# A reordered hybrid encoder trunk: one token piece loaded by ScalarE, two diagonals made on ScalarE, the third input block in full width, and a new order table

## The chip, the cores and the metric

The kernel runs on one core of a Trainium2 chip. The metric is the device time of one execution in microseconds (us), lower is better. The times below are medians of several executions, and one execution was taken by the hardware profiler.

## What is computed

One layer of an encoder for 512 tokens of 1024 channels, in float32. In short, from the reference:

```python
h = rmsnorm(x, mix_norm)
p = h @ w_in                                  # 3072 + 3072 + 1024 + 32 + 2048 columns, cut in parts:
rx, ry, qkv, z, ba, gates = split(p)
y_rg = rglru_branch(rx, ry, ...)              # conv, gates r and i, a = exp(..r), scan both ways, * gelu(ry)
y_dn = deltanet_branch(qkv, z, ba, ...)       # conv, chunks of 64, triangular solve, state, gated norm, both ways
g = sigmoid(gates)
x = x + (g1 * (y_rg @ w_rnn_proj) + g2 * (y_dn @ w_dn_proj)) @ w_out
x = x + (silu(u) * v) @ w_down                # u, v = rmsnorm(x, ffn_norm) @ w_gate_up, D_FF = 2816
out = rmsnorm(x, final_norm)
```

Here rmsnorm multiplies every token by the reciprocal root of its mean square and every channel by a gain.

## The kernel before

**Layout and numbers.** Tokens are columns in most of the kernel: a matrix of channels by tokens. A float32 factor is split in a high part of fewer bits (type fp32r, made by a cast or a scaled copy) and the remainder, and a product is made of three products: high by high, high by low and low by high. For a block of 128 output channels of the input projection that makes 24 matrix products of 512 columns (`mm3`, 8 slices of 128 input channels by three), or, with `parts=2`, 48 products of 256 columns: first all 24 for one half of the tokens, then all for the other. Some large products (z, the gate and up projections, w_out) go by a scheme of seven products on sums of blocks in place of eight; the sums of weight blocks are made by a transfer that POOL (GpSimd) issues and that adds a block in memory to a tile (`t<-t` on POOL).

**Stages.** The tokens are loaded, squared, scaled by the gain and transposed on TensorE (PE). The first products, for z, use the tokens with the gain but without the reciprocal root, which is applied to the result. Meanwhile the roots are found: `rows_of` builds for each of the two token tiles of a pair a diagonal matrix of the reciprocal roots (ident times rin) and multiplies it by ones on PE, so that every partition holds the row of factors (tile r), which `scaled_parts` uses to make the normalised tokens hh (high) and hl (low). The first block that reads hh is the small block ba. Then follow the RG-LRU branch in four groups of three blocks of 128 channels (its last decay-gate ACTIVATE starts at 250 us), the DeltaNet branch in four groups of two heads, the output projections, the FFN and the final norm.

**What sets the order.** The kernel's functions don't emit instructions. V, A, G, T and Q are recorders (class `Rec`) of DVE (VectorE), ACT (ScalarE), POOL, PE and SP, and each call is noted with a number. `Plan.emit` then emits all recorded operations in the order of a long table of numbers, ORDER (lines 31 to 425); a second table, HOMES (lines 426 to 466), says which buffer each tile of the pools t2, t4 and ps gets, and a tile waits for the last use of what its buffer held. Every engine works through its own instructions in that order. Since all are emitted in one line, all rows of a profile of this kernel carry the line L517, and are told apart by the names and forms of their tiles.

**Names.** In the profile, t is any tile of the pools t2 and t4, ps a bank of the accumulators. With numbers, in the order: t211_88 and t212_89 are the first and the second half (512 channels each) of token tile 0, t213_90 and t214_91 those of token tile 1; t4522, t4525, t4530 and t4533 are weight pieces of z; t421 and t422 the first two high parts of the scaled tokens (without root), ps25 to ps28 the banks in which the tokens are transposed; t241 the diagonals; ps520 and ps521 the first results of z. Later t4582 is a weight block, t4583 and t4584 its cast and the cast's copy with the sign turned, which the in-memory sums use. Near the end ps1781 and ps1786 are 256-column quarters of the last result, ps1779 and ps1785 halves of 512 columns.

**Where the change sits.** The token loads go out on SP, the order of the loop is tile 0 first half, tile 1 first half, then the second halves, and the only transfer that ACT issues in the first microseconds is that of the gain. The squares of t211_88 and t213_90 are made by ACT, those of the second halves by DVE. `in_proj` is called for one block after another, counts them in `first_tiles`, and gives `mm3` two parts while fewer than three are done.

Of the kernel before, what the change touches and what calls it, by code (L numbers as in the profile page):

```python
# [9 lines left out]
AF = mybir.ActivationFunctionType  # L10
ALU = mybir.AluOpType
# [3 lines left out]
P = 128  # L15
# [507 lines left out]
def trunk(ctx: ExitStack, tc: tile.TileContext, x, mix_norm, w_in, rg_conv_w, rg_conv_b, rg_wa, rg_ba, rg_wx, rg_bx,  # L523
# [129 lines left out]
    def rows_of(rins):  # L653
        diag, pr, r = two(shape=(P, 2, P)), axb(), two(shape=(P, 256))
        for i, rin in enumerate(rins):
            V.tensor_scalar(diag[:, i, :], ident, rin, None, ALU.mult)
            T.matmul(pr[:, i * P:(i + 1) * P], ones, diag[:, i, :], start=True, stop=True)
# [1268 lines left out]
```

## Time and profile before

| what | value |
|---|---|
| median of 3 executions | 1045.61 us (1044.15 to 1045.66) |
| the profiled execution | 1045.31 us |
| its span in the trace | 1043.6 us |
| TensorE clock granted, mean | 0.999 |
| bytes read and written | 133.18 and 18.91 MB |
| instructions counted | 18109 |

Times in the profile are microseconds from the start of the span. A row of a timeline has the start, the duration, the engine, the line, the operation, the tiles (out<-in), the shapes and how many like it followed each other; in brackets stands how long the engine was idle before it and what it waited for. A row of the waits view gives the tile whose instruction waited, what was waited for, the total, the number and the longest. PEld is the weight load of TensorE, SPq, ACTq and POOLq are issues of transfers.

### The profile page before, as it was taken

The numbers are of one execution on the slowest core, as the hardware profiler recorded it, in microseconds if no ns is written. First come the engines' busy times: TensorE is split into PE (matmuls) and PEld (weight loads), VectorE is DVE, ScalarE is ACT, GpSimd is POOL, SyncE is SP. The second block draws the span as 40 slices with busy tenths as digits, with TensorE's granted clock in tenths as the row PEclk, the third lists the DMA queues.
The fourth block names the chain that finished last, engine by engine and source line by source line (L and its number), as shares of the span: only waits on it lengthen the run. The fifth ranks groups of instructions, "written<-read, shape, count | busy, mean of one in ns | idle before, by whom it ended". The sixth has DMA issues, their size and how long they took to land.

```text
span 1043.6 us, 18109 instructions
## 1 busy us (share of the span) xinstructions
PE 1031.2 (99%) x6699; PEld 902.5 (86%) x6699; DVE 909.2 (87%) x1701; ACT 726.7 (70%) x1325; POOL 97.5 (9%) x145
## 2 busy tenths in 40 slices
PE   8999999999999999999999999999999999999997
PEld 7988888888888898897788888889999999998886
DVE  6899999958986489768958969999999998999998
ACT  7789999898447567986987564678544454445674
POOL 6000000214000032241212000000000000000000
PEclk9999999999999999999999999999999999999999
DMA  9942523525515227898974645795473533265622
GB/s 288 310 158 87 165 76 84 132 70 150 128 51 158 57 70 208 203 206 202 274 182 106 173 138 188 249 302 180 144 240 122 152 87 87 80 202 161 221 102 81
DMA packets 185512, 163.75 MB, mean 157 GB/s; under 512 B 7728, under 2 KB 156352, under 8 KB 185424
## 3 DMA queue, kind: packets, MB, share of 16 engines
q1 hardware_dynamic: 178896, 144.63, 46.2%
q0 software_dynamic: 5344, 14.82, 7.8%
q10 hardware_dynamic: 1184, 3.15, 0.8%
q8 instruction: 52, 0.85, 0.3%
q14 instruction: 36, 0.29, 0.1%
HBM read 133.18 MB, written 18.91 MB: 146 GB/s over the span
## 4 chain that ended last, share of the span: by engine, by line
PE 87%; DMA 4%; ACT 4%; DVE 2%; issue 2%; SPq 0%; DVEq 0%; POOLq 0%; ACTq 0%
PE ps L517 87%; ACT t L517 3%; DMA t<-in_w_in_dram 2%; DVE t L517 2%; DMA t<-t 1%; ACT L517 1%; ACT ps L517 1%; DMA zs<-t 0%; SPq L517 0%; DVE na L517 0%; ACT drt L517 0%; ACT rst L517 0%; DVEq L1921 0%; DVE rin L517 0%; POOLq L517 0%
## 5 line engine op out<-in xcount | busy, mean ns | idle before, releaser
L517 PE MATMUL ps<-t,t 128*128 128x512 f32 (+3 forms) x3039 | 538.5, 321 | 2.2 <-DMA t<-t 1.4
L517 DVE TENSOR_TENSOR t<-t,t 128x512 fp32r<-128x512 f32 (+19 forms) x807 | 508.7, 662 | 35.2 <-PE ps L517 13.8
L517 PEld LDWEIGHTS ps<-t,t 128*128 128x128 f32 (+1 forms) x3039 | 432.4, 179 | 60.4 <-DMA t<-t 1.8
L517 PE MATMUL ps<-hh,t 128*128 128x512 f32 (+2 forms) x1696 | 459.0, 346 | 0.8 <-ACT t L517 0.6
L517 ACT CAST t<-t 128x512 fp32r<-128x512 f32 (+2 forms) x400 | 299.1, 781 | 169.2 <-DVE t L517 67.3
L517 PEld LDWEIGHTS ps<-hh,t 128*128 128x128 f32 (+1 forms) x1696 | 301.0, 189 | 40.7 <-ACT t L517 1.5
L517 PE MATMUL ps<-hl,t 128*128 128x512 f32 (+2 forms) x856 | 280.6, 346 | 0.0
L517 PEld LDWEIGHTS ps<-hl,t 128*128 128x128 f32 (+1 forms) x856 | 159.6, 188 | 18.6
L517 ACT ACT_TABLE_LOAD x69 | 88.5, 1283 | 5.9 <-DVE so L517 3.1
L517 DVE SCALAR_TENSOR_TENSOR t<-ps,par,t 128x511 f32<-128x511 f32 (+1 forms) x108 | 79.2, 744 | 11.2 <-ACT t L517 9.9
L517 ACT COPY t<-ps 128x512 f32<-128x512 f32 (+3 forms) x108 | 44.5, 429 | 56.3 <-PE ps L517 51.2
L517 ACT ACTIVATE t<-t 128x128 f32<-128x128 f32 (+5 forms) x114 | 72.6, 647 | 7.3 <-DVE t L517 6.2
L517 DVE TENSOR_TENSOR t<-ps,t 128x256 f32<-128x256 f32 (+1 forms) x106 | 50.7, 487 | 14.1 <-PE ps L517 12.3
L517 ACT ACTIVATE t<-ps,par 128x512 f32<-128x512 f32 x68 | 46.3, 705 | 10.0 <-PE ps L517 9.4
L517 DVE TENSOR_TENSOR t<-t 128x512 f32<-128x512 f32 (+1 forms) x81 | 51.4, 643 | 0.3
L517 ACT ACTIVATE t<-ps 128x512 f32<-128x512 f32 (+1 forms) x58 | 29.3, 509 | 23.4 <-PE ps L517 21.7
L517 PE MATMUL ps<-t,na 128*128 128x128 f32 (+2 forms) x640 | 44.2, 232 | 0.1
L517 PEld LDWEIGHTS ps<-t,na 128*128 128x128 f32 (+2 forms) x640 | 40.0, 145 | 3.8 <-issue 1.6
L517 POOL TENSOR_SCALAR_AFFINE_SELECT t<-t 128x512 f32<-128x512 f32 x32 | 24.7, 777 | 193.1 <-DMA t<-gcr 168.2
L517 PE MATMUL ps<-ident,t 128*128 128x128 f32 (+1 forms) x200 | 31.8, 275 | 1.3 <-DMA t<-in_x_dram 0.7
L517 POOL TENSOR_SCALAR t<-t,dnse 128x128 f32<-128x128 f32 x48 | 29.5, 768 | 38.9 <-ACT ps L517 23.9
L517 POOL DMA_DIRECT2D t<-t x20 | 17.4, 871 | 152.5 <-ACT t L517 129.0
(151 smaller groups left out, 598.3 us busy)
## 6 DMA issues: line engine op xcount, KB each, us to landing
t<-in_w_in_dram SPq DMA_DIRECT2D x70, 512.0 KB, 5.8
t<-in_w_gate_up_dram SPq DMA_DIRECT2D x44, 512.0 KB, 4.8
t<-in_w_down_dram SPq DMA_DIRECT2D x22, 512.0 KB, 5.1
t<-t POOLq DMA_DIRECT2D x20, 512.0 KB, 6.4
t<-in_w_down_dram SPq DMA_DIRECT2D x33, 256.0 KB, 3.9
t<-in_w_out_dram SPq DMA_DIRECT2D x12, 512.0 KB, 6.5
t<-in_w_rnn_proj_dram SPq DMA_DIRECT2D x16, 384.0 KB, 4.2
sums<-t SPq DMA_DIRECT2D x11, 512.0 KB, 5.6
```

The costliest lines, as they stand in the source:

```text
L517: self.plan.ops.append((self.eng, {x.tensor.name for x in aps}, outs, lambda: real(*a, **kw)))
```

## The change

Three functions are edited, and both tables are replaced.

```diff
@@ rows_of
         for i, rin in enumerate(rins):
-            V.tensor_scalar(diag[:, i, :], ident, rin, None, ALU.mult)
+            A.activation(diag[:, i, :], ident, AF.Copy, scale=rin)
             T.matmul(pr[:, i * P:(i + 1) * P], ones, diag[:, i, :], start=True, stop=True)
@@ trunk, the token loads
         for c in range(2):
-            Q.dma_start(xl_[c][h], x[0, c * P:(c + 1) * P, 512 * h:512 * h + 512])
+            (A if c and not h else Q).dma_start(xl_[c][h], x[0, c * P:(c + 1) * P, 512 * h:512 * h + 512])
@@ in_proj
-        mm3(po, hi, lo, lambda k: hh[:, k, :], lambda k: hl[:, k, :], KD, 2 if len(first_tiles) < 3 else 1)
+        mm3(po, hi, lo, lambda k: hh[:, k, :], lambda k: hl[:, k, :], KD, 2 if len(first_tiles) < 2 else 1)
@@ ORDER = """ (all numbers replaced; the first of each)
-2 17 18 19 20 21 22 23 24 25 26 27 28 29 0 3 5 2085 10 14 11 7 15 9 16 2086 1 12 13 66 67 6 2103 2104 2087 65 33 34 35
...
```

One of the four token loads, tile 1's first half, moves to ACT's queue. The two diagonals are made by ACT as a copy scaled by rin. The third block of the input projection is made with 24 products of 512 columns in place of 48 of 256. In number of instructions PE has 24 products fewer, DVE two operations fewer, ACT two ACTIVATEs, one transfer and four table loads more (73 for 69), SP one transfer fewer; the rest is the same work in another order and in other buffers. Lines of the changed kernel stand one lower, L516 for L517.

The head of SP's order, before and then now:

```order
L517 DMA t4522_599<-in_w_in_dram 128x512
L517 DMA t211_88<-in_x_dram 128x512
L517 DMA t213_90<-in_x_dram 128x512
L517 DMA t4522_599<-in_w_in_dram 128x512
L517 DMA t212_89<-in_x_dram 128x512
L517 DMA t214_91<-in_x_dram 128x512
```
```order
L516 DMA t4522_599<-in_w_in_dram 128x512 x2
L516 DMA t211_88<-in_x_dram 128x512
L516 DMA t4525_602<-in_w_in_dram 128x512
L516 DMA t212_89<-in_x_dram 128x512
L516 DMA t214_91<-in_x_dram 128x512
```

The second piece of the first weight moved ahead of the first token piece, a third weight piece ahead of the second halves, and t213_90 left this queue. The head of ACT's order, before and now:

```order
L517 DMA gain1r15_92<-in_mix_norm_dram 8x128
L517 ACT_TABLE_LOAD
L517 ACTIVATE warm10_87<-eps_t9_86 128x1
L517 CAST t4523_600<-t4522_599 128x512
L517 ACTIVATE t233_110,ssq29_106<-t211_88 128x512
L517 CAST t4523_600<-t4522_599 128x512
L517 ACTIVATE t421_98<-ps25_102,gain117_94 128x256
L517 ACTIVATE t239_116,ssq35_112<-t213_90 128x512
L517 ACTIVATE t421_98<-ps25_102,gain117_94 128x256
```
```order
L516 DMA t213_90<-in_x_dram 128x512
L516 DMA gain1r15_92<-in_mix_norm_dram 8x128
L516 ACT_TABLE_LOAD
L516 CAST t4523_600<-t4522_599 128x512
L516 ACT_TABLE_LOAD
L516 ACTIVATE warm10_87<-eps_t9_86 128x1
L516 CAST t4523_600<-t4522_599 128x512
L516 ACTIVATE t233_110,ssq29_106<-t211_88 128x512
L516 ACTIVATE t239_116,ssq35_112<-t213_90 128x512
L516 ACTIVATE t421_98<-ps25_102,gain117_94 128x256 x2
```

Both casts of the first weight and both squares now stand ahead of the first scaled half (t421). Further on in ACT's order the diagonals (t241) stand between scaled halves:

```order
L516 ACTIVATE rst37_114<-ssq35_112,ssh36_113 128x1
L516 ACTIVATE t241_118<-ident1_78,rin32_109 128x128
L516 ACTIVATE t422_99<-ps27_104,gain117_94 128x256
L516 ACTIVATE t241_118<-ident1_78,rin38_115 128x128
L516 CAST t4531_608<-t4530_607 128x512
```

On PE all sixteen transposes of the tokens stood ahead of the first product of z; now only the eight of t211_88 and t213_90 do, eight products follow, then the eight transposes of t212_89 and t214_91. In the middle (about 480 us), ACT's order around the cast and the copy of the weight block t4582, before and then now:

```order
L517 CAST t4583_660<-t4582_659 128x1024
L517 ACTIVATE t4584_661<-t4583_660 128x1024
L517 CAST t4593_670<-t4546_623 128x1024
L517 ACTIVATE t2770_847,so767_844<-t4736_813 128x128
L517 ACT_TABLE_LOAD
```
```order
L516 CAST t4583_660<-t4582_659 128x1024
L516 ACTIVATE t2770_847,so767_844<-t4736_813 128x128
L516 COPY t2850_927<-na841_918 32x256 x4
L516 COPY t4518_595<-ps551_628 128x512
L516 CAST t4591_668<-t4541_618 128x1024
L516 ACTIVATE t41056_1133<-t41055_1132 128x1024
L516 COPY t4518_595<-ps552_629 128x512
L516 ACTIVATE t2771_848,so767_844<-t4736_813 128x128
L516 ACTIVATE t2770_847,so767_844<-t4736_813 128x128
L516 ACTIVATE t4584_661<-t4583_660 128x1024
```

The copy t4584 stood right behind its cast; now eight rows stand between. The end of PE's order, before and now, the products of the down projection into the last banks:

```order
L517 MATMUL ps1786_1863<-t41971_2048,t41977_2054 128x256
L517 MATMUL ps1781_1858<-t41956_2033,t41960_2037 128x256
L517 MATMUL ps1781_1858<-t41955_2032,t41961_2038 128x256
L517 MATMUL ps1781_1858<-t41963_2040,t41968_2045 128x256
L517 MATMUL ps1781_1858<-t41964_2041,t41968_2045 128x256
L517 MATMUL ps1781_1858<-t41963_2040,t41969_2046 128x256
L517 MATMUL ps1781_1858<-t41971_2048,t41976_2053 128x256
L517 MATMUL ps1781_1858<-t41972_2049,t41976_2053 128x256
L517 MATMUL ps1781_1858<-t41971_2048,t41977_2054 128x256
```
```order
L516 MATMUL ps1779_1856<-t41971_2048,t41976_2053 128x512
L516 MATMUL ps1779_1856<-t41972_2049,t41976_2053 128x512
L516 MATMUL ps1779_1856<-t41971_2048,t41977_2054 128x512
L516 MATMUL ps1785_1862<-t41971_2048,t41976_2053 128x512
L516 MATMUL ps1785_1862<-t41972_2049,t41976_2053 128x512
L516 MATMUL ps1785_1862<-t41971_2048,t41977_2054 128x512
```

Before, token tile 1's quarter of 256 columns came last; now it is token tile 0's half of 512 columns.

862 rows, old and new, of tables (HOMES, ORDER) are left out of this document.

## Prediction

> **What bounds the kernel now.** I read the page's busy shares first, then what TensorE (PE) waits for, then the same by stage, and last the timelines of the places where PE stops. The busy shares of the page:
>
> ```profile
> PE 1031.2 (99%) x6699; PEld 902.5 (86%) x6699; DVE 909.2 (87%) x1701; ACT 726.7 (70%) x1325; POOL 97.5 (9%) x145
> ```
>
> PE works 1031.2 of the span's 1043.6 us, so only 12.4 us of the span lie outside PE's work, and no order of the same work can bring more than that. A part of it is the end, after the last product. The waits of PE over the whole span (in total, times, longest):
>
> ```profile
> PE ps L517 <- DMA t<-t: 1.6, 2, 1.4
> PE ps L517 <- ACT t L517: 1.2, 2, 0.7
> PE ps L517 <- POOL eps_t L517: 1.1, 1, 1.1
> PE ps L517 <- DVE t L517: 0.8, 1, 0.8
> PE ps L517 <- DMA t<-in_x_dram: 0.7, 2, 0.5
> PE ps L517 <- issue: 0.6, 1, 0.6
> ```
>
> Asked for 480 to 560 us alone, the same view gives the first two rows unchanged and no other: 2.8 us of the 6.0 that have a name lie there. The waits for the constant eps_t, for x and for VectorE (DVE) lie in the first 15 us, 2.6 us. Two stretches of the windows view (length; then busy time of PE, PEld, DVE, ScalarE (ACT), POOL) say where the other engines are near their own limit:
>
> ```profile
> 70.00:250.00 180.00, 180.00 (x814) 148.91 (x813) 160.51 (x202) 164.17 (x256) 19.11 (x24) 1.00 0.39 104
> 480.00:560.00 80.00, 77.03 (x627) 64.56 (x626) 60.80 (x163) 70.00 (x142) 15.31 (x26) 1.00 0.75 191
> ```
>
> In the recurrent part PE never stops, but ACT has only 15.8 us free of 180. From 480 to 560 PE stops for 3.0 us, DMA is busiest there, 0.75, and ACT is 70.00 of 80 busy.
>
> **The change, part by part: the start.** The timelines of PE, ACT, DVE, POOL and SP there (start, duration, instruction):
>
> ```profile
> 5.64 0.33 PE L517 MATMUL ps<-ident,t 128*128 128x128 f32 x1
> 6.42 0.66 PE L517 MATMUL ps<-ident,t 128*128 128x128 f32 x4 [0.45 <-DMA t<-in_x_dram]
> 8.78 0.87 PE L517 MATMUL ps<-ident,t 128*128 128x128 f32 x6
> 9.41 4.07 PE L517 MATMUL ps<-t,t 128*128 128x512 f32 x15
> 14.30 0.71 PE L517 MATMUL ps<-t,ones 128*128 128x128 f32 x4 [0.81 <-DVE t L517]
> 14.77 7.53 PE L517 MATMUL ps<-t,t 128*128 128x512 f32 x32
> 22.14 0.40 PE L517 MATMUL ps<-hh,t 128*64 128x256 f32 x2
> 30.74 0.88 PE L517 MATMUL ps<-hh,t 128*128 128x256 f32 x6
> ```
> ```profile
> 1.42 1.28 ACT L517 ACT_TABLE_LOAD   x1 [1.42 <-PEq L1912]
> 2.72 0.20 ACT L517 ACTIVATE warm<-eps_t 128x1 f32<-128x1 f32 x1
> 3.94 0.62 ACT L517 CAST t<-t 128x512 fp32r<-128x512 f32 x1 [1.03 <-DMA t<-in_w_in_dram]
> 7.47 0.62 ACT L517 CAST t<-t 128x512 fp32r<-128x512 f32 x1 [2.17 <-DMA t<-in_w_in_dram]
> 8.36 0.62 ACT L517 ACTIVATE t<-t 128x512 f32<-128x512 f32 x1
> 8.97 0.83 ACT L517 ACTIVATE t<-ps,gain 128x256 fp32r<-128x256 f32 x2
> ```
> ```profile
> 8.10 0.69 DVE L517 SCALAR_TENSOR_TENSOR t<-t 128x512 f32<-128x512 f32 x1 [2.18 <-DMA t<-in_x_dram]
> 11.96 2.29 DVE L517 TENSOR_SCALAR t<-ident,rin 128x128 f32<-128x128 f32 x2
> ```
> ```profile
> 10.39 7.53 POOL L517 TENSOR_TENSOR t<-t,t 128x512 fp32r<-128x512 f32 x6 [0.47 <-ACT t L517]
> ```
> ```profile
> 1.25 0.89 SPq L517 DMA_DIRECT2D t<-in_x_dram  x2
> ```
>
> A pitch is the distance of like instructions in a row: (22.14-14.77)/32 = 0.230 us for a product of 512 columns, (0.88-0.40)/4 = 0.120 for 256 columns (runs of six and of two), (9.41-8.78)/6 = 0.105 for a transpose.
>
> *Token pieces.* SP issues the halves of the first token pair 0.45 us apart, yet the transposes of the first start by 5.64 and those of the second wait until 6.42. In the old queue order (weight, x, x, weight, x, x) the pieces of 256 KB are seen in use at 3.94, by 5.64, 6.42, 7.47, 8.10 and 8.78: one piece after the other, at the pace of bytes. The new order of issue is weight and t213_90 (on ACT's queue, at the same time), weight, t211_88. Counted in bytes, t211_88 is now the fourth piece, at 7.47 instead of 5.64 or before: the label "token tiles first" does not hold for it. If ACT's piece goes beside the others, it is the third, at 6.42. The Trainium skill (DMA: Bandwidth & Descriptors, "Issuing engines are not separate DMA queues") says that transfers from several issuers share the same 16 DMA engines, and that a second issuer saves only issue time; by it the later time holds, and the sum is as I take it below. I take 7.47, which the old arrivals, paced by bytes, are nearest to.
>
> *First product.* Behind that piece ACT now does both squares (8.97-8.36 = 0.61 each), then the first scaled half, half of the 0.83 for two: 7.47+1.22+0.42 = 9.11, against 9.41 before. The added ACT issue and table load lie in the time before 7.47, in which ACT waits 1.03 and 2.17 us; one load more is 1.28, so they cost nothing unless the second weight comes before they end.
>
> *Diagonals.* The two on DVE took 2.29 us, while POOL was working in 10.39 to 17.92, and PE waited 0.81 for them. On ACT a scaled copy of twice the width takes 0.42 in a pair, which bounds a diagonal from above, and the warm-up of one column, 0.20, from below: I take 0.3. Behind the waiting diagonals on ACT stand the scaled halves of the tokens' second half and the casts of the third and fourth weight piece. Adding ACT's rows from 7.47 in the new order (two squares, five scaled halves, three casts at 0.62, two roots at 0.20, two diagonals) gives 7.47+1.22+2.08+1.86+0.40+0.60 = 13.6 for the second one; PE comes to them after 18 products and 8 transposes, at 9.11+4.14+0.84 = 14.1. No wait is left there, by a margin of 0.5 that holds only while the token pieces come no later than taken.
>
> *Sum of the start.* From the first product to the block ba, the first to read normalised tokens: 48 products x 0.230 = 11.04, the eight transposes that now stand among them 0.84, the diagonals' records 14.77-14.30 = 0.47, together 12.35. So ba would start at 9.11+12.35 = 21.46 against 22.14: **-0.7 us**. With t211_88 third it is 1.05 earlier, -1.7. In before, 22.14-9.41 = 12.73 holds 11.51 of that work and 1.22 of stalls; if as much comes back, it is +0.5. These are the ends.
>
> **Third block uncut.** 24 products of 512 columns in place of 48 of 256: 24 x (2 x 0.120 - 0.230) = **-0.24 us**, on PE, so on the path. Since its second half of tokens is now needed at once and not 24 products (2.9 us) later, a wait of up to 2.9 for it bounds it on the other side; the blocks before it have read these tokens already, so I take none.
>
> **The middle.** The longest wait of PE with a releaser is a chain; the rows are of ACT, POOL and PE:
>
> ```profile
> 482.50 1.06 ACT L517 CAST t<-t 128x1024 fp32r<-128x1024 f32 x1 [2.55 <-DMA t<-in_w_in_dram]
> 483.59 1.06 ACT L517 ACTIVATE t<-t 128x1024 fp32r<-128x1024 f32 x1
> ```
> ```profile
> 485.30 0.85 POOL L517 DMA_DIRECT2D t<-t  x1 [5.76 <-ACT t L517]
> ```
> ```profile
> 492.56 1.42 PE L517 MATMUL ps<-t,t 128*128 128x512 f32 x5 [1.40 <-DMA t<-t]
> 510.27 0.50 PE L517 MATMUL ps<-hh,t 128*128 128x512 f32 x1 [0.19 <-DMA t<-t]
> ```
>
> A weight block comes late (ACT waits 2.55), its cast and negated copy follow at once, POOL adds another block to it by DMA at 485.30, and PE waits 1.40 for the sum. I laid both orders along PE's own products at the pitches above: between the issue of that weight's load (t4582) and POOL's DMA stood 7.7 us of products, now 13.6; for the pair behind 510.27 it is 8.2 before and 16.8 after from POOL's DMA to the first product. That is 5.9 and 8.6 us of room for waits of 1.40 and 0.19. On ACT eight rows now stand between cast and copy of t4584, at the cast's 1.06 us each at most 8.5 us, which is more than the 5.9; but four are copies of 32 rows by 256 columns and two of 128 columns, so I count about half, and 1.5 to 2 us of the room stay. Against this stands that the table is new for every instruction: of the tight spots that it makes I see none for certain, but ACT stays 70 of 80 busy. The ends are all 2.8 and the 0.6 of issue won, -3.4, and as much lost again as is there now, +3. I take half of the gain, **-1.5 us**.
>
> **The end.** The last rows of DVE, ACT and PE:
>
> ```profile
> 1032.63 4.91 PE L517 MATMUL ps<-t,t 128*128 128x512 f32 x29
> 1033.55 0.64 ACT L517 ACTIVATE t<-na 128x512 f32<-128x512 f32 x1 [0.28 <-DVE na L517]
> 1034.09 0.19 ACT L517 ACTIVATION_READ_ACCUMULATOR t<-na 128x1 f32 x1
> 1036.62 0.69 DVE L517 TENSOR_TENSOR na<-ps,na 128x512 f32<-128x512 f32 x1
> 1037.58 0.42 DVE L517 TENSOR_TENSOR na<-ps,na 128x256 f32<-128x256 f32 x1 [0.26 <-PE ps L517]
> 1038.04 0.42 DVE L517 SCALAR_TENSOR_TENSOR t<-na 128x256 f32<-128x256 f32 x1
> 1039.12 0.72 ACT L517 ACTIVATE t<-t,rin 128x512 f32<-128x512 f32 x1 [0.23 <-DVE rin L517]
> ```
>
> PE ends at 1037.54; a quarter of 256 columns is added in 0.42 and squared in 0.42 on DVE, and the scaling starts 1.58 us after PE's end. In the new order a half of 512 columns is last: added in 0.69, then squared on ACT in 0.64, its sum read in 0.19 more. That is 0.27 and about 0.3 longer (0.1 of the read overlaps, as 1033.55+0.64 against 1034.09 shows): **+0.6 us**, ends 0.3 (the square in quarters on DVE) and 0.8.
>
> **Sum.** -0.68 - 0.24 - 1.5 + 0.6 = -1.8 against the profiled execution of 1045.31: **1043.5 us**. The median of the runs shown, 1045.61, is 0.30 above that execution; a measurement of this kernel tells about 0.2%, 2.1 us, from no change, so "faster" begins at 1043.5, and my figure lies on that line. The likeliest case alone spans 1042.0 to 1045.0: start and middle each half-way to their lower ends (0.5 and 1.0 less), and three tenths of the way up to the higher ones (0.4 and 1.3 more).
>
> **Rivals.** *All waits go.* The start's early variant, -1.7, all of the middle, -3.4, -0.24 and +0.6: -4.7, 1040.6. For it speaks that each of the two waits shown has gained more room than it is long; against it that no order so far left PE without a wait where DMA is 0.75 busy. 0.22 (1040.6 to 1042.0).
>
> *The waits only move.* New tight places take back the 1.5 of the middle, and the rest is -0.3: 1045.0. For it: the table is new throughout. 0.20.
>
> *ACT becomes the bound of the recurrent part: slower.* The table loads in 70 to 250 us before, a row of the groups by line (busy, mean ns):
>
> ```profile
> L517 ACT ACT_TABLE_LOAD x25 | 32.1, 1283 | 0.4
> ```
>
> In the new order 35 loads, in place of 31, stand ahead of the last decay-gate ACTIVATE (the one that reads rgs): 4 x 1.283 = 5.1 us more on an engine that has 15.8 free, beside a PE that has no idle time to give. It decides where a group of three blocks has no ACT slack left, that is where its loads eat more than their part of the 15.8. If half of it shows, 1045.31+2.6-0.3 = 1047.6 without a gain in the middle; if all, 1050.1. Against it: 5.1 is a third of what is free. The Trainium skill (ScalarE: Activation LUTs, "What ACT_TABLE_LOAD costs") puts a drain of 1.38 us to each load, which would make it 10.6 us. Here no run shows that drain: the load of 1.42 ended at 2.70 and the next ACTIVATE began at 2.72. 0.13.
>
> **How the numbers follow.** Forecast 0.45, all waits go 0.22, waits move 0.20, ACT bound 0.13. Half of the forecast's chance lies below 1043.5: faster 0.22+0.22 = 0.44, same 0.23+0.20 = 0.43, slower 0.13. The range runs from 1040.8 to 1047.6, which leaves out most of the ACT case and a little at the lower end.
>
> **What would show it.** Right: the block ba at about 21.5, no wait of PE for the diagonals, the waits of 480 to 560 at 1.3 or less, PE's busy time shorter by 0.24 and 0.6 more after its last product. Wrong: t211_88 in use before 6.4, waits of PE for ACT anywhere in 70 to 250, or new waits for DMA above 2 us elsewhere.

## The result, and the profile after

The changed kernel takes 1039.59 us (median of 4 runs, 1038.58 to 1040.61) against 1045.63 for the kernel before: a ratio of 0.9944, 95% interval 0.9927 to 0.9961. That is 6.0 us less where 1.8 to 2.1 was forecast, and below the range. In two later groups of runs, those of the experiments, each on a chip of its own, the kernel before itself came out at 1043.84 and 1043.71 and the changed one at 1040.55 and 1039.42, both times a ratio of 0.9963 (0.9951 to 0.9976, 0.9950 to 0.9975). The three intervals overlap between 0.9951 and 0.9961, so a lead of 4 to 5 us fits all of them, and the 6.0 of the first group is not confirmed. The profiled execution took 1040.44 us, with a span of 1038.7.

The busy shares, the waits of TensorE over the whole span, and the two stretches of the windows view, 70 to 250 and 480 to 560 us:

```profile
PE 1028.2 (99%) x6675; PEld 902.0 (87%) x6675; DVE 906.1 (87%) x1699; ACT 730.5 (70%) x1331; POOL 91.1 (9%) x145
```
```profile
PE ps L516 <- issue: 1.6, 1, 1.6
PE ps L516 <- POOL ones L516: 1.1, 1, 1.1
PE ps L516 <- ACT t L516: 0.9, 1, 0.9
PE ps L516 <- DVE t L516: 0.3, 1, 0.3
```
```profile
70.00:250.00 180.00, 180.00 (x814) 148.78 (x813) 161.77 (x200) 171.49 (x265) 13.70 (x23) 1.00 0.36 104
...
480.00:560.00 80.00, 80.00 (x647) 68.87 (x646) 64.19 (x178) 70.29 (x151) 13.25 (x19) 1.00 0.80 204
```

Every wait for a transfer and all of the 2.8 us between 480 and 560 are gone; PE is busy for 80.00 of 80. In the recurrent part ACT now works 171.49 of 180 us; 5.1 of the 7.3 more are its four table loads. PE still never stops there. The DMA share of the second stretch is 0.80, higher than before, and yet PE has no wait there; that no order had managed this was the prediction's point against "all waits go". A new row is the first, 1.6 us in which PE waits for nothing that the profile shows.

The second thing to see is the busy time itself. It fell by 3.0 us, and the 24 products fewer explain 0.24 of that. The ends of products are modelled: a product of 512 columns that stands alone has a record of 0.39 us where the pitch is 0.23, so a wait of up to 0.16 us behind it counts as its work. Busy time is not the sum of the work, and the 12.4 us that lay outside it before were no bound on what an order can win. The Trainium skill says so in its own way (Perfetto Trace Analysis, "Summary: the profiler window per engine type": the end of a TensorE row is an estimate), and the traces agree: the kernel after_third_cut below has PE make the same 6699 products as the kernel before, in the new order, and is busy for 1027.6 us instead of 1031.2.

The start, PE and then ACT:

```profile
6.75 0.60 PE L516 MATMUL ps<-ident,t 128*128 128x128 f32 x4
9.03 2.12 PE L516 MATMUL ps<-t,t 128*128 128x512 f32 x8 [0.93 <-ACT t L516]
14.16 0.61 PE L516 MATMUL ps<-t,ones 128*128 128x128 f32 x4
14.53 7.09 PE L516 MATMUL ps<-t,t 128*128 128x512 f32 x30
21.45 0.28 PE L516 MATMUL ps<-hh,t 128*64 128x256 f32 x1
```
```profile
4.74 0.62 ACT L516 CAST t<-t 128x512 fp32r<-128x512 f32 x1 [1.60 <-DMA t<-in_w_in_dram]
7.29 0.62 ACT L516 ACTIVATE t<-t 128x512 f32<-128x512 f32 x1
13.29 0.39 ACT L516 ACTIVATE t<-ident,rin 128x128 f32<-128x128 f32 x1
```

The block ba starts at 21.45, 0.69 earlier than before, and PE has no wait at the diagonals (14.16). The end, PE's last row and the last scaling on ACT:

```profile
1025.67 6.49 PE L516 MATMUL ps<-t,t 128*128 128x512 f32 x32
...
1034.20 0.72 ACT L516 ACTIVATE t<-t,rin 128x512 f32<-128x512 f32 x1 [0.23 <-DVE rin L516]
```

PE ends at 1032.16 and the span 6.54 later; before it was 1037.54 and 6.06. So the end costs 0.5, and PE is 5.38 us ahead at its end: 0.69 from the start, 0.24 from the uncut block, and 4.4 from somewhere between 22 and 1032. By that part the prediction was wrong. DeltaNet's first 32x32 products of each group of heads are marks that both orders have; rows of PE for the second, third and fourth group in the kernel before, then after:

```profile
426.68 0.75 PE L517 MATMUL ps<-t,na 32*32 32x32 f32 x64
...
517.53 0.75 PE L517 MATMUL ps<-t,na 32*32 32x32 f32 x64
...
600.92 0.75 PE L517 MATMUL ps<-t,na 32*32 32x32 f32 x64
```
```profile
424.41 0.75 PE L516 MATMUL ps<-t,na 32*32 32x32 f32 x64
...
513.60 0.75 PE L516 MATMUL ps<-t,na 32*32 32x32 f32 x64
...
594.90 0.75 PE L516 MATMUL ps<-t,na 32*32 32x32 f32 x64
```

A mark that comes earlier is a gain only if as much work stands ahead of it. Counted in the traces, and apart from the uncut block, the new order has four products of 512 columns more ahead of the second mark (1590-24 for 1562), six fewer ahead of the third (1856-24 for 1838) and equally many ahead of the fourth, there with seven of 128 columns fewer. With these and the 0.93 of start and uncut block taken off, PE is ahead by 2.2 us at the second mark, 1.6 at the third and 4.3 at the fourth. So the 4.4 is there by 595 us, and half of it before 424 us, in a stretch where the profile before has one wait of PE, 0.6 us.

The products of the third mark read what a long serial chain of small DVE operations makes. Its first and last large transpose on DVE, before and after:

```profile
480.26 1.18 DVE L517 STREAM_TRANSPOSE t<-t 128x512 f32<-128x512 f32 x1
...
516.62 0.71 DVE L517 STREAM_TRANSPOSE t<-t 128x512 f32<-128x512 f32 x1
```
```profile
477.29 1.20 DVE L516 STREAM_TRANSPOSE t<-t 128x512 f32<-128x512 f32 x1
...
511.78 0.71 DVE L516 STREAM_TRANSPOSE t<-t 128x512 f32<-128x512 f32 x1
```

The chain now begins 3.0 us earlier and is done 4.8 us earlier. Between these rows DVE makes 84 operations in both orders; before, two of them wait for PE, 1.44 and 0.31 us, the first right behind PE's own wait of 1.40 for a weight at 492.56, and after, none does. The mark stands 0.2 us behind the chain's end before and 1.1 after.

### The profile page after: what moved, and what is told of

The parts are those of the page before. It is cut to its first block, busy times and chain, and to the rows that moved or that the text cites. A ratio compares the mean times of both kernels' runs of the same rounds, so it can differ in the third digit from the quotient of the medians.

```text
span 1038.7 us, 18051 instructions
## 1 busy us (share of the span) xinstructions
PE 1028.2 (99%) x6675; PEld 902.0 (87%) x6675; DVE 906.1 (87%) x1699; ACT 730.5 (70%) x1331; POOL 91.1 (9%) x145
## 4 chain that ended last, share of the span: by engine, by line
PE 98%; ACT 1%; DMA 0%; issue 0%; DVE 0%; ACTq 0%; DVEq 0%
PE ps L516 98%; ACT t L516 1%; DMA t<-in_w_in_dram 0%; ACTq L516 0%; DVE t L516 0%; ACT L516 0%; DVE na L516 0%; DVEq L1920 0%; DVE so L516 0%; ACT so L516 0%; ACT rst L516 0%; ACT warm L516 0%; DVE rin L516 0%
## 5 line engine op out<-in xcount | busy, mean ns | idle before, releaser
L516 PE MATMUL ps<-t,t 128*128 128x512 f32 (+3 forms) x3039 | 536.0, 322 | 2.5 <-issue 1.6
L516 DVE TENSOR_TENSOR t<-t,t 128x512 fp32r<-128x512 f32 (+19 forms) x807 | 506.3, 658 | 27.8 <-ACT t L516 13.4
L516 PEld LDWEIGHTS ps<-t,t 128*128 128x128 f32 (+1 forms) x3039 | 430.6, 180 | 58.2 <-issue 2.7
L516 PE MATMUL ps<-hh,t 128*128 128x512 f32 (+2 forms) x1680 | 456.5, 347 | 0.0
L516 ACT CAST t<-t 128x512 fp32r<-128x512 f32 (+2 forms) x400 | 298.0, 780 | 158.9 <-DVE t L516 60.5
L516 PEld LDWEIGHTS ps<-hh,t 128*128 128x128 f32 (+1 forms) x1680 | 298.1, 189 | 38.2 <-ACT t L516 0.2
L516 PE MATMUL ps<-hl,t 128*128 128x512 f32 (+2 forms) x848 | 278.6, 347 | 0.0
L516 PEld LDWEIGHTS ps<-hl,t 128*128 128x128 f32 (+1 forms) x848 | 158.4, 189 | 19.5 <-issue 0.2
L516 DVE SCALAR_TENSOR_TENSOR t<-ps,par,t 128x511 f32<-128x511 f32 (+1 forms) x108 | 79.3, 744 | 14.7 <-ACT t L516 13.7
L516 ACT COPY t<-ps 128x512 f32<-128x512 f32 (+3 forms) x108 | 44.3, 429 | 52.7 <-PE ps L516 51.4
L516 ACT ACTIVATE t<-t 128x128 f32<-128x128 f32 (+5 forms) x114 | 72.6, 647 | 9.8 <-DVE t L516 8.0
L516 DVE TENSOR_TENSOR t<-ps,t 128x256 f32<-128x256 f32 (+1 forms) x106 | 50.3, 486 | 11.4 <-PE ps L516 8.7
L516 DVE TENSOR_TENSOR t<-t 128x512 f32<-128x512 f32 (+1 forms) x81 | 51.0, 636 | 0.9 <-DMA t<-in_w_out_dram 0.6
L516 ACT ACTIVATE t<-ps,par 128x512 f32<-128x512 f32 x68 | 45.8, 707 | 7.4 <-PE ps L516 7.2
L516 POOL TENSOR_SCALAR_AFFINE_SELECT t<-t 128x512 f32<-128x512 f32 x32 | 25.6, 807 | 218.5 <-DMA t<-gcr 107.5
L516 PE MATMUL ps<-t,na 128*128 128x128 f32 (+2 forms) x640 | 42.9, 232 | 0.0
L516 PEld LDWEIGHTS ps<-t,na 128*128 128x128 f32 (+2 forms) x640 | 39.6, 145 | 3.8 <-issue 1.4
L516 ACT ACTIVATE t<-ps 128x512 f32<-128x512 f32 (+1 forms) x58 | 28.7, 508 | 15.5 <-PE ps L516 15.0
L516 PE MATMUL ps<-ident,t 128*128 128x128 f32 (+1 forms) x200 | 32.4, 276 | 0.3 <-DVE t L516 0.3
L516 POOL DMA_DIRECT2D t<-t x20 | 18.1, 938 | 146.4 <-ACT t L516 131.3
L516 DVE SCALAR_TENSOR_TENSOR t<-ps,negc,t 128x128 f32<-128x128 f32 x48 | 13.7, 344 | 19.0 <-PE ps L516 18.9
```

Source lines behind the costliest of these rows:

```text
L516: self.plan.ops.append((self.eng, {x.tensor.name for x in aps}, outs, lambda: real(*a, **kw)))
```

## The experiments

Times are medians in us; a ratio is to the kernel before in the same group. The theory at first was that the new order wins, not the edits of functions, and that it wins by weights that come earlier; the rivals are with each run.

**order_alone: the new tables with the old functions.** The three edits undone, the new tables kept (the third block's 48 products in the places of the 24):

```diff
-            A.activation(diag[:, i, :], ident, AF.Copy, scale=rin)
+            V.tensor_scalar(diag[:, i, :], ident, rin, None, ALU.mult)
-            (A if c and not h else Q).dma_start(...)
+            Q.dma_start(...)
-        mm3(..., KD, 2 if len(first_tiles) < 2 else 1)
+        mm3(..., KD, 2 if len(first_tiles) < 3 else 1)
```

> The three edits of functions undone (all token loads on SP, the diagonals on VectorE, the third block in two halves of 256 columns), the new tables kept. Theory 'order': the gain of the changed kernel lies in the new table, above all in the waits of TensorE between 470 and 570 us that are gone; then this kernel is within 2 us of the changed one, 1039 to 1042 us, slower by the 0.24 us of the uncut block and up to 1 us of waiting for diagonals. Rival 'edits': the start and the uncut block bring it; then it is near 1045.

1041.71, ratio 0.998 (0.9969 to 0.9991). The waits of 480 to 560 us stayed away, but ba started only at 23.30. So the new tables bring about 2 us without any edit. (ORDER and HOMES were exchanged together; which of the two matters was not tried.)

**start_edits_alone: the old tables with the two edits of the start.**

```diff
-            V.tensor_scalar(diag[:, i, :], ident, rin, None, ALU.mult)
+            A.activation(diag[:, i, :], ident, AF.Copy, scale=rin)
-            Q.dma_start(...)
+            (A if c and not h else Q).dma_start(...)
```

> The kernel before with its own tables, and only the two edits of the start: the diagonals on ScalarE, and the first half of token tile 1 loaded by ScalarE's queue. Theory 'order': only the start can gain, at most the 0.81 us that TensorE waited for the diagonals and a part of the 0.7 for x; 1044.0 to 1045.6 us. Rival 'edits': 1041 or less.

1043.33, ratio 1.0000 (0.9988 to 1.0011). In its profile ba started at 21.22, 0.9 us earlier than before, and the time is the same: with the old tables the two edits bring nothing. With the new tables they bring some 2 us, though compared across groups: after_third_cut below has order_alone's tables and these two edits, with ratios of 0.9959 and 0.9955 in its two runs. So it is neither alone; the earlier start counts only in the new order. The place of the waits had moved, too; a row of PE:

```profile
509.40 0.50 PE L517 MATMUL ps<-hh,t 128*128 128x512 f32 x1 [1.79 <-DMA t<-t]
```

This wait was 0.19 in the profile before, and the one at 492.56, 1.40 there, is not seen here: with another start another weight is the late one. DVE's chain was done at 514.30 here, 3.0 us earlier than before, and yet the mark stands at 516.66, 0.9 earlier, because PE itself came late.

**after_diag_dve and after_x_sp: one edit undone each.**

```diff
-            A.activation(diag[:, i, :], ident, AF.Copy, scale=rin)
+            V.tensor_scalar(diag[:, i, :], ident, rin, None, ALU.mult)
```

> The changed kernel with the two diagonals back on VectorE at their places in the new order. By the prediction's own step they take 2.29 us there beside GpSimd's work, so they end near 15.2 us where TensorE wants them at 14.2: a wait of about 1 us and the block ba at about 22.4 in place of 21.45; time +1.0 us. Rival: VectorE has more room in the new order and the diagonals come in time: +0.2 or less.

```diff
-            (A if c and not h else Q).dma_start(...)
+            Q.dma_start(...)
```

> The changed kernel with all four token loads on SP, t213_90 now third of the token and weight pieces behind t211_88. If pieces come at the pace of bytes whatever queue issues them, t211_88 is one piece earlier and t213_90 one or two later than in the changed kernel, the second square on ScalarE starts later, and the block ba moves by 0 to +0.7 us; if the second queue brings its piece beside the others, +0.7 to +1.2.

With the diagonals on DVE 1042.11, ratio 0.9981 (0.9972 to 0.9989), against 0.9963 of the changed kernel in other groups and 0.9961 of after_x_sp in its own: about 2 us worse, twice what was expected. The rows of PE show that the wait is not one but several, and that ba starts 1.6 us later:

```profile
14.61 0.49 PE L516 MATMUL ps<-t,ones 128*128 128x128 f32 x2 [0.16 <-DVE t L516]
...
21.66 1.20 PE L516 MATMUL ps<-t,t 128*128 128x512 f32 x4 [0.29 <-DVE t L516]
23.05 0.34 PE L516 MATMUL ps<-hh,t 128*64 128x256 f32 x1 [0.20 <-DVE t L516]
```

With all token loads on SP 1040.13, ratio 0.9961 (0.9949 to 0.9973): the same as the changed kernel, with ba at 21.30. A second queue brought nothing. The rule of the Trainium skill quoted in the prediction, that a second issuer saves only issue time, holds here.

**after_control, before_early_loads and after_late_loads: are late weights the cause?** The first is the changed kernel itself. The other two only move loads in ORDER (operation numbers in words):

```diff
 before_early_loads: SP's loads of t41054, t4582, t4915, t4920, t4928, t41034, t4943
-  where the table has them
+  each right behind the last use of what its buffer held
 after_late_loads: SP's loads of t41054, t4582, t4915, t4943
-  where the table has them
+  each right ahead of its cast on ACT
```

> The changed kernel itself, unedited, run beside the others of this group, so that they can be compared with it on one chip. If its lead over the kernel before is the one measured first, 0.994 to 0.995 of it.

> The kernel before with seven weight loads between 440 and 600 us (t41054, t4582, t4915, t4920, t4928, t41034, t4943) moved up in its order to right behind the last use of what their buffers held; nothing else is changed. Theory 'late weights': the waits of TensorE between 480 and 560 us come from these loads; they shrink to 1 us or less and the time falls by 2 to 4 us. Rival 'not the loads': the waits come from ScalarE's order or from the transfers being slow there; they stay, and the time is the same within 1 us.

> The changed kernel with four weight loads (t41054, t4582, t4915, t4943) moved down in its order to right ahead of their casts, as t4915 stood in the kernel before. Theory 'late weights': ScalarE waits some 4 to 6 us for each, as for those 12.0 us in all before, and TensorE waits again between 470 and 570 us; time +2 to +5 us against the changed kernel. Rival 'not the loads': other work covers it, TensorE's waits stay under 0.5 us, time the same within 0.5.

after_control 1040.55, ratio 0.9963 (0.9951 to 0.9976), less of a lead than the 0.994 to 0.995 expected. before_early_loads 1047.39, ratio 1.0039 (1.0024 to 1.0054): slower, where 2 to 4 us less were expected. The waits for weights went, and two others came; rows of DVE and PE:

```profile
495.72 0.69 DVE L503 TENSOR_TENSOR t<-t,t 128x512 f32<-128x512 f32 x1 [3.56 <-DMA t<-in_w_out_dram]
```
```profile
517.67 0.94 PE L503 MATMUL ps<-t,na 32*32 32x32 f32 x64 [3.09 <-DVE t L503]
```

The loads moved up stand ahead of one of w_out, for which DVE now waits. And the 32x32 products begin at 517.67, where they began at 517.53 without a wait: PE came there 3 us earlier and waited for DVE's chain. Behind that wait the trace has TensorE's clock at one half for 3.41 us, from 517.95; that is a part of what this run lost (see the last section). The theory of late weights alone fell. after_late_loads 1042.18, ratio 0.9986 (0.9977 to 0.9996), 1.6 us above its control, with waits of PE for ACT near 530 (1.17 and 0.34 by its rows): late loads do cost, but less than the 2 to 5 us expected.

**before_early_loads2, before_dve_more, after_dve_more: two limits?** The new theory was that weights and DVE's chain are late by about the same in the kernel before. The second and third run do one DVE addition of that stretch five times:

```diff
 before_early_loads2: before_early_loads, and SP's load t4836 (w_out) ahead of t4915
 before_dve_more (after_dve_more: 3822)
+        plan.ops += [plan.ops[3846]] * 4
         plan.emit()
```

> As before_early_loads, but the load of w_out (t4836), for which VectorE waited 3.56 us there, moved up as well, ahead of t4915. New theory 'two limits': in the kernel before, TensorE's waits for weights (near 492 and 510 us) and VectorE's serial chain of small operations, whose end lets TensorE's 32x32 products begin at 517.5 us, are late by nearly the same amount, so that neither alone is worth anything. Here VectorE's chain begins earlier by the 1.4 us that it no longer waits for TensorE and TensorE has no wait for weights: the 32x32 products begin near 515.5 to 516.5, with a wait for VectorE of 1 to 2 us in front; time 1 to 2 us below before. Rival 'late weights alone': no wait is left and the time is 2.5 to 4 us below. Rival 'transfers': moving loads up only delays others, the time is that of before or above.

> The kernel before with one VectorE addition of the w_out sums (t4837 from t4835, 128x512, about 0.61 us in a row) done five times instead of once, at its place ahead of the end of the serial chain; the result is not changed. 'Two limits': the chain has no slack, TensorE's wait at the 32x32 products near 517 us becomes 1.8 to 2.4 us, time +1.8 to +2.4. Rival 'late weights alone': VectorE has room there, +0.5 or less.

> The changed kernel with the same addition done five times. There the chain's last transpose ends at 512.5 and TensorE begins the 32x32 products at 513.6 without a wait: about 1 us of slack. 'Two limits': wait of 1.0 to 1.6 us, time +1.0 to +1.6 against the changed kernel. Rival: more slack than that, +0.3 or less.

before_early_loads2 1043.53, ratio 0.9999 (0.9991 to 1.0008): the same. Its 32x32 products began at 515.55, 2 us earlier as expected, without the wait for DVE that was expected in front, and the time did not follow: waits of 0.55 for ACT and 1.21 for DVE stand behind them, near 525 and 528 us. before_dve_more 1045.58, ratio 1.0016 (1.0007 to 1.0024), 1.8 us above before, as expected; after_dve_more 1042.45, ratio 0.9985 (0.9976 to 0.9994) against 0.9963 in other groups, some 2.3 us and more than expected. There, too, the trace has the half clock for 3.41 us right behind the wait, from 514.60. The waits at the mark, before and after:

```profile
518.47 0.75 PE L503 MATMUL ps<-t,na 32*32 32x32 f32 x64 [1.17 <-DVE t L503]
```
```profile
513.79 0.75 PE L502 MATMUL ps<-t,na 32*32 32x32 f32 x64 [1.80 <-DVE t L502]
```

So DVE's chain has little room in both kernels: four additions more, some 2.7 us of DVE's time by its busy time in the chain, cost 1.8 and about 2.3 us, the latter with the slow clock in it.

**before_sums_pool, before_both, before_chain_first, before_chain_loads: the chain moved.** Three additions taken off DVE, then with the earlier loads; and the chain's start put as the new order has it, without and with the earlier loads:

```diff
 before_sums_pool (before_both: in before_early_loads2)
-        V.tensor_tensor(s_[:, 0, :], ra[:, 0, :], ra[:, 1, :], ALU.add)
+        E = G if len(plan.ops) == 3846 else V
+        E.tensor_tensor(s_[:, 0, :], ra[:, 0, :], ra[:, 1, :], ALU.add)
 ...
 before_chain_first (before_chain_loads: in before_early_loads2)
-  ACT: cast t4591, copy t41056, then the last three copies t2850
+  ACT: the last three copies t2850, then cast t4591, copy t41056
-  DVE: t4592, t4538, t4517, transpose t2852, t4538, t2573, transpose t4851
+  DVE: transpose t2852, t4592, transpose t4851, t2853, t4538, t4517, t4538, t2573
```

> The kernel before with three additions of the w_out sums (t4837, t4836) that stood in VectorE's queue ahead of its serial chain made by GpSimd instead, which waited 11.8 us just there. 'Two limits': VectorE's chain ends up to 1.9 us earlier, but TensorE's waits for weights stay, so 0 to -0.8 us. Rival 'the chain alone is the limit': -1.5 to -2 us. Rival 'shared port': both engines slow each other, +0.5 or more.

> before_early_loads2 (eight loads moved up) together with the additions on GpSimd of before_sums_pool: both limits moved. 'Two limits': the 32x32 products begin near 513.5 to 514.5 instead of 517.5 us and the time falls by 1.5 to 3 us below before, more than the two alone add up to. Rival 'what is gained there is lost behind it': the products begin early, and new waits of TensorE for ScalarE and VectorE between 520 and 560 us take it back, 0 to -0.8 us.

> The kernel before with only the start of VectorE's serial chain near 475 us put as the new order has it: on ScalarE the cast of t4541, which waited 1.42 us for its weight, and the copy t41056 go behind the three copies of the state (t2850) instead of ahead of them; on VectorE the chain's two first transposes go ahead of the sum t4592 and of z's combination. 'Two limits, set by the chain's start': the chain begins 2 to 3 us earlier than 480.26, TensorE keeps its waits for weights, so 0 to -1 us. Rival 'the chain alone is the limit': -2 us or more. Rival 'nothing local brings it': the same within 0.5 us or above.

> before_chain_first with the eight earlier loads of before_early_loads2. 'Two limits, set by the chain's start': TensorE comes to the 32x32 products at 514.2 as in before_early_loads, and finds the chain done or within 1 us of it; they begin at 514 to 515 instead of 517.5 us and the time falls by 2 to 3 us. Rival 'what is gained there is lost behind it': they begin early, new waits between 520 and 560 us take it back, 0 to -0.8 us.

before_sums_pool 1044.10, ratio 1.0004 (0.9996 to 1.0013); before_both 1044.95, 1.0017 (1.0008 to 1.0026); before_chain_first 1043.31, 0.9995 (0.9986 to 1.0004); before_chain_loads 1044.40, 1.0003 (0.9993 to 1.0013). None is faster than the kernel before by more than the noise, two limits moved together are not either (before_both is slower), and with that the second theory fell as a full cause. The rows of before_chain_loads, first DVE, then PE's waits between 500 and 560 us, show how:

```profile
476.20 1.20 DVE L503 STREAM_TRANSPOSE t<-t 128x512 f32<-128x512 f32 x1
...
514.04 0.71 DVE L503 STREAM_TRANSPOSE t<-t 128x512 f32<-128x512 f32 x1
```
```profile
PE ps L503 <- DMA t<-t: 1.2, 1, 1.2
PE ps L503 <- DVE t L503: 1.1, 1, 1.1
PE ps L503 <- ACT t L503: 0.7, 1, 0.7
```

The chain began 4.1 us earlier than before. Yet the 32x32 products began at 515.99, only 1.5 us earlier: the chain took 38.6 us from its first to its last large transpose, against 37.1 before and 35.2 in the changed kernel. The two transposes had been put ahead of other sums, and so three more operations, 87 in place of 84, now stood inside the chain. The new order has the earlier start with 84. And 3.0 us of waits, for a transfer, DVE and ACT, stand around and behind the mark.

**after_third_cut, after_third_cut_again, after_code_shift, after_control2: the stop near 427 us.** The stop of 1.6 us in the changed kernel, rows of PE, and of the transfers in 425 to 428.5 us the row of code:

```profile
426.14 0.79 PE L516 MATMUL ps<-t,t 32*32 32x32 f32 x62
428.53 0.67 PE L516 MATMUL ps<-t,t 32*32 32x32 f32 x34 [1.60 <-issue]
```
```profile
q8 instruction: 1, 0.02, 1.7%
```

96 small products that run in about 1.2 us without a stop are cut after 62, and one code transfer runs just then. The trace has it at 426.12 for 0.96 us. In all seven profiles with this stop the one code transfer begins between 0.3 us ahead of and 0.4 us behind the first of the 96 products, and the stop ends 1.2 to 1.5 us behind the end of that transfer; in the four profiles of the new order without it, the same piece had come by 422.5 us. The edits: the third block back in halves; and, in after_code_shift, twelve 32x32 products near 330 us made twice, for the same number of instructions more:

```diff
 after_third_cut (and again)
-        mm3(..., KD, 2 if len(first_tiles) < 2 else 1)
+        mm3(..., KD, 2 if len(first_tiles) < 3 else 1)
 after_code_shift (the twelve first operations on ps615, each repeated right behind itself)
+        plan.ops += [plan.ops[i] for i in [...]]
         plan.emit()
```

> The changed kernel with the third input block back in two halves, 48 products of 256 columns in the place of 24 of 512. By the products alone +0.24 us. But the profile of the changed kernel has TensorE idle for 1.6 us near 427 us with nothing waited for, while a code transfer is under way, at the same instruction in three kernels, and not in the kernel with the new order and the old functions, whose code on TensorE is 48 instructions longer ahead of that place. Theory 'code loading': where the code's pieces end decides that stop, so here it is gone, and the time is 1.4 us lower or more; rival: the stop has another cause and stays, +0.2 us.

> The changed kernel with the third block in two halves, once more, since it came out lowest: if the stop of TensorE for code near 427 us is what it lacks, again 1038.5 to 1039.5 us, and no such stop in its profile.

> The changed kernel itself once more, as the yardstick of this group: 1040 to 1041 us, with the stop of TensorE for code near 427 us in its profile.

> The changed kernel in which twelve of the first 32x32 products of the DeltaNet branch (near 330 us) are each made twice, with the same result: 48 instructions more on TensorE, as many as the uncut block has fewer, ahead of the place near 427 us, and some 0.2 us of products. Theory 'code loading': the stop at 427 us goes, as with the third block cut, and the time falls by 1.2 to 2 us. Rival 'the cut block': the gain of after_third_cut came from its products standing otherwise; then the stop stays, +0.2 us.

after_third_cut 1038.77, ratio 0.9959 (0.9944 to 0.9973), 1.8 us below its control by the medians; again 1038.79, 0.9955 (0.9940 to 0.9970). after_code_shift 1038.72, 0.9955 (0.9941 to 0.9969), against after_control2 1039.42, 0.9963 (0.9950 to 0.9975; 1040 to 1041 was expected of it): 0.7 us and less than the 1.2 to 2 expected. Of after_code_shift, the rows of PE and its waits over the whole span:

```profile
426.32 1.16 PE L502 MATMUL ps<-t,t 32*32 32x32 f32 x96
...
510.75 0.75 PE L502 MATMUL ps<-t,na 32*32 32x32 f32 x64
```
```profile
PE ps L502 <- POOL ones L502: 1.1, 1, 1.1
PE ps L502 <- ACT t L502: 0.9, 1, 0.9
PE ps L502 <- DVE t L502: 0.3, 1, 0.3
```

The 96 products run through, and the mark that stood at 513.60 stands at 510.75; the span is 1036.8 against 1038.9 of its control. Seven profiles with the code of the changed kernel at that place have the stop (1.3 to 2.1 us), the four that are 48 instructions longer have none there. So where code ends up decides it, and not what the third block does. What it is worth is not settled: 0.7 to 1.8 us by the medians, 0.4 to 0.8 by the ratios, whose intervals overlap. after_third_cut and after_code_shift have the lowest medians found; the fourth without the stop is order_alone, whose start is late. The absence of the stop is not all either: the profiled execution of after_third_cut took 1040.57 us, with a wait of 1.82 for DVE at 525.07 that the second profile of the same kernel does not have.

## Why the prediction was wrong

**The bound** failed in its first step: PE's time outside its busy time, 12.4 us, was taken for all that an order can win. Busy time fell by 3.0 us with 0.24 us of work less. The forecast's lower end of the middle, -3.4, was made of named waits only and inherits the error, and so does the rival that came nearest, "all waits go".

**The start** was right in its sum, in part by luck. Forecast: first product at 9.11, diagonals done at 13.6, ba at 21.46. Measured: 9.03, 13.68 (13.29+0.39), 21.45. That ACT is what PE waits for at the first product is the 0.93 in front of 9.03. Not right was the arrival: t211_88 is in use at 6.75, not 7.47, and the first weight comes at 4.74, 0.8 later than before. From then until the first scaled half ACT works without a break, so the second table load, taken as free, is in the way: the casts and that load took up what the earlier token piece gave, and two errors cancelled. Nor is 0.69 a fixed size: ba stands between 21.54 and 22.43 in the eight profiles with the old tables and the old start, and between 21.27 and 21.66 in the eight with the new tables and both edits, 0.5 apart in the mean.

**The uncut block** was forecast at -0.24, and by its products it is that. What was not seen is that 48 instructions less shift the code, which put a stop of 1.6 us near 427 us; with the block cut again the kernel is no slower (after_third_cut).

**The middle** is the step that failed: "I take half of the gain, -1.5 us". All the 2.8 us of waits between 480 and 560 went, and the whole stretch from 22 us to PE's end brought 4.4 in the profiled execution, with the stop of 1.6 us and the slow clock behind it (below) already paid from it. Without them, by after_code_shift's profiled span against that of its control, it is some 6.5. The term was sized from the waits that the profile names, most of them between 480 and 560 us; about half of the 4.4 was won before 424 us, where hardly any stand. Room counted in PE's products between a load and its use was the reason given; moving only the loads showed that this reason is too narrow, since it gave nothing in the kernel before and cost 1.6 in the changed one. One reading in it was off, too: the eight rows between cast and copy of t4584 hold eleven instructions and took 5.8 us (473.77 to 479.60), more than the half of 8.5 that was counted; POOL's DMA behind them went out at 481.22 all the same, 4.1 us earlier than before.

Shown is: the new tables and the two edits of the start win only together the full 4 us or more; DVE's chain has little room at the third mark in both kernels (before_dve_more, after_dve_more); and in the new order it starts 3.0 us earlier and runs without waits. Not shown is which of the moves make that. Earlier loads, work taken off DVE and an earlier start of the chain were tried alone and in pairs. In five of these six runs the mark came 1.5 to 2.4 us earlier, in before_early_loads 0.1 later, and the time never fell clear of the noise. What fits all runs is that the kernel before has several limits close together between 475 and 560 us (weights, ACT's copies, DVE's chain, w_out's loads) and that only an order that moves all of them wins; that remains an argument. What wins the 2 us before 424 us was not looked into.

**The end** was right: +0.6 forecast, +0.5 measured. **ACT as a bound** of the recurrent part fell: 171.49 of 180 us busy, and no wait of PE between 20 and 250 us. **Waits only move**, the middle rival, is what happened to every local move in the kernel before, and not to the change itself. Of the signs that the prediction named for being right, all came but one: PE's busy time fell by 3.0, not 0.24, and that is where the missing gain lay.

A part of the miss may be no step of the working: in both later groups the same two kernels differ by a ratio of 0.9963, which would be 1041.7 from 1045.6 and inside the range. That lead of 3.9 us is still about twice the forecast one.

## What to carry to other kernels

A busy share of 99% on the engine with modelled ends is not a bound: compare a mark that both programs have, such as a row of unlike shape, read how much earlier it comes, and count what work stands ahead of it in each. A wait is worth its length only if nothing else is due at the same moment, so before costing a wait's removal, ask at its place which other engine's chain ends there, and test that by adding work to it. When nothing in a profile explains a stop within a run of very short instructions, look at the code transfers, and try a harmless shift of the code.

## What the runs showed of the hardware

Code is fetched in pieces of 16 KB while the kernel runs, 52 of them in the changed kernel, in 0.9 to 1.8 us each by the trace's own records. In 32x32 products PE runs through its code fast (96 in 1.16 us), and in the seven profiles where a piece was fetched just as such a run began, PE stood still for 1.3 to 2.1 us. Whether the load on the DMA engines (1.04 in 427 to 429 us) plays a part was not tried.

The stop can cost more than itself. Two rows of the windows view of the changed kernel, 427 to 429 and 429 to 432.4 us; the column behind the five engines is the granted clock:

```profile
427.00:429.00 2.00, 0.47 (x34) 0.47 (x34) 2.00 (x4) 0.83 (x2) 0.00 (x0) 0.89 1.04 243
429.00:432.40 3.40, 3.40 (x27) 2.52 (x14) 3.12 (x7) 2.89 (x8) 0.00 (x0) 0.56 1.11 257
```

After 1.6 us of standing still the mean granted clock of the second stretch was 0.56; the trace has it at one half from 428.56 for 3.41 us. PE's products of 512 columns in it:

```profile
430.25 2.12 PE L516 MATMUL ps<-t,t 128*128 128x512 f32 x5
```

That is a pitch of (2.12-0.39)/4 = 0.43 us in place of 0.23, so such a spell costs about 1.6 us, an estimate from these two pitches. Four of the seven profiles with the stop have the spell; after_diag_dve, after_late_loads and after_dve_more had the stop without it. The same 3.41 us at half clock stand behind the waits in front of the third mark in before_early_loads (3.09 us), after_dve_more (1.80) and before_both (1.54). The Trainium skill (TensorE: Matmul & The Clock Gate, "HAM oscillation — how this bites in real kernels") gives as the rule that idle gaps above about 3.4 us bring the half clock. Here gaps of 1.5 to 3.1 us beside very short products were enough, in some runs; the measurement decides. The length of the slow spell, 3.4 us, agrees with the window of which that page of the Trainium skill speaks.
